# Two-layer encoder in one kernel: the two ends of the seven-product feed-forward cycle in a new order

## Chip, cores and metric

The kernel runs on one core of a Trainium2 chip. The metric is the device time of one launch in microseconds (us). The time before is 1501.56 us, the median of three runs (1500.29, 1501.56 and 1502.72 us).

## The reference, cut to what matters

Two layers over 512 tokens of width 1024. Each layer has three parts, each followed by a layer norm of `ALPHA * x + y`:

```
for l in range(DEPTH):
    y = hybrid_mixer(x, ...)                      # latent attention beside a convolution
    x = layer_norm(ALPHA * x + y, ln1_g[l], ln1_b[l])
    y = memory_cross_attention(x, mem, ...)       # 4 heads of 256, 256 memory tokens
    x = layer_norm(ALPHA * x + y, ln2_g[l], ln2_b[l])
    y = swiglu_ffn(x, ffn_w_in[l], ffn_w_down[l]) # hidden width 2816
    x = layer_norm(ALPHA * x + y, ln3_g[l], ln3_b[l])

def memory_cross_attention(...):
    s = einsum(q, k) * scale;  p = softmax(s);  return einsum(p, v) @ w_o
def swiglu_ffn(x, w_in, w_down):
    g, up = halves of x @ w_in;  return (silu(g) * up) @ w_down
```

## The kernel before, in words

**Numbers.** Every float32 matrix is split into a high and a low part (`split`: ACT writes the high part, DVE subtracts it to get the low part). A product is three matmuls in a row, high by high, low by high, high by low (`mm3`, L250, L251, L252). Tiles named whi, xsh, hs, ph, yx are operands' high parts or pairs, wlo, xsl, pl their low parts.

**Weights.** A raw 512 KB weight tile is fetched by SP (`fetch`) into one of 3 raw buffers. ACT casts it to the high part (L287, L606), ACT writes minus the high part into the low tile (L288, L607), and a DMA issued by POOL adds the raw tensor to it in flight (L289, L608: `wlo<-in_fdn`, `wlo<-in_fin`). There are 7 such pairs of tiles; PSUM has four banks accb, three psb and one convb (every fourth request for a psb bank gets convb).

**Cross attention.** `scores(q, kv)` is 24 matmuls and a softmax on DVE and ACT; `turn(p)` transposes the probabilities on PE (L1242), 8 in all, and splits them (ph, pl); `mix` multiplies them with the values. `first_half(u)`, u = 0 to 3, are the four parts of the first half of the output projection. Before, the order is: scores of head 2, first_half(0), turn of head 2, scores of head 3, first_half(1).

**Feed-forward input.** gate and up are computed in 22 pairs of 128 features (`Pair`), each by seven products instead of eight, on halves of tokens and of width. The token operands are seven: 11 and 21 (`first`) and 22, t1, t2, t4, t3 (`sums`), each made for two chains of token tiles (t = 0 and 1; their halves share one operand tile): t1 = b12 - b11, t2 = b22 - t1, t4 = b21 - t2, t3 = b22 - b12. POOL computes these differences (tsum, L564), PE transposes each in four blocks (`put`, L550), ACT casts (xsh, L225), DVE subtracts (xsl, L226). The weight operands are likewise sums of the pair's gate and up halves (ssum, L619 to L628 on DVE), cast by ACT (L640) with the low part from DVE (L645). A product is 12 matmuls of 256 columns. Its names: p1, p2 (into one accb half), p67, p3, p45; `copy1`, `early_sums`, `late_sums` and `hidden` combine them (DVE), with a tanh on ACT (L688).

`tail_pairs` makes the second half of the attention output, its layer norm (with POOL's ve and rstd, L450, L454) and, in a block of fixed order, the token operands, with p1 and p2 of pairs 0 to 2 between them. `ffn` then runs 22 cycles. In cycle j the sums and casts of pair j+1 are made, and hidden(j-1) is finished.

**Down projection.** For each of 22 feature tiles, `operands(j)` makes the weight tile (`added_weights`) and the hidden tile's split (hs), and `step` issues 24 matmuls of 512 columns (4 token tiles, 2 halves, 3 parts).

**What sets the order.** Inside `with issue_order(...)` the instructions of PE, DVE, ACT, POOL and SP stand in the order in which the code is written; each engine executes its own list in that order, and waits by semaphores. Outside it a scheduler places them by priority. SP's list is a DMA queue of its own, POOL's another.

## Time and profile before

The profiled execution took 1502.71 us. Its span was 1500.9 us, at a mean granted TensorE clock of 0.983.

| engine | busy us | share | instructions |
|---|---|---|---|
| PE (matmul) | 1433.6 | 96% | 9647 |
| DVE | 1023.4 | 68% | 1749 |
| ACT | 804.7 | 54% | 1500 |
| POOL | 500.9 | 33% | 695 |

An engine's busy time is the sum over its instructions. The rest of the span is waiting, and a wait on PE is put down to the instruction whose end released it. PE's busy time also holds matmuls that run at half clock: 0.5 in the column PEclk means 1.2 GHz, 1.0 means 2.4 GHz. The second layer repeats the first about 737.5 us later.

### The profile page before, as it was taken

Reading aid. Unit: us, or ns where it says so; the run is one execution under the profiler, and the core shown is the slowest. Engines: PE = TensorE matmul, PEld = TensorE weight load, DVE = VectorE, ACT = ScalarE, POOL = GpSimd, SP = SyncE. Lnnn points to the kernel's source line nnn. Section 1 sums busy time; section 2 is a strip of 40 time slices with the busy share of each in tenths; the row PEclk is TensorE's granted clock in tenths of the full one; section 3 lists DMA queues with packets and bytes.
Section 4 is the critical chain, followed back from the end, with each engine's and each line's share of the span. In section 5 each row is a group of like instructions: output and inputs, shape, how many; then the busy total and the mean of one; then the engine's idle time right before and its main releaser. Section 6 shows DMA issues by size and latency. Waiting matters only on the chain.

```text
span 1500.9 us, 25060 instructions
## 1 busy us (share of the span) xinstructions
PE 1433.6 (96%) x9647; PEld 1311.2 (87%) x9647; DVE 1023.4 (68%) x1749; ACT 804.7 (54%) x1500; POOL 500.9 (33%) x695
## 2 busy tenths in 40 slices
PE   8899999999799999899999999999997999998997
PEld 8799988988699999888889998888886999997886
DVE  7999677565588888620469986785566888884205
ACT  4667773352356656663146777534415656655630
POOL 2789762001511111211157987410023111111211
PEclk9999999999899999999999999999998999999999
DMA  5434343252477887999433444423525878789971
GB/s 178 152 102 147 108 166 98 94 160 71 112 180 181 183 182 187 256 264 220 120 107 121 141 122 123 150 84 113 155 71 134 194 177 189 181 182 291 252 142 56
DMA packets 68504, 230.67 MB, mean 154 GB/s; under 512 B 7776, under 2 KB 7808, under 8 KB 68384
## 3 DMA queue, kind: packets, MB, share of 16 engines
q1 hardware_dynamic: 45632, 158.09, 32.3%
q0 software_dynamic: 22752, 70.98, 24.9%
q8 instruction: 76, 1.25, 0.3%
q14 instruction: 44, 0.36, 0.1%
HBM read 212.26 MB, written 12.58 MB: 150 GB/s over the span
## 4 chain that ended last, share of the span: by engine, by line
PE 70%; DVE 10%; DMA 7%; ACT 5%; issue 4%; POOL 4%; SPq 0%; POOLq 0%; DVEq 0%; ACTq 0%
PE accb L250 12%; PE accb L251 11%; PE accb L252 11%; PE psb L250 9%; PE psb L251 9%; PE psb L252 9%; DMA raw<-in_xo 3%; PE convb L250 2%; PE convb L252 2%; PE convb L251 2%; DVE convb L844 2%; DMA raw<-in_fdn 1%; DVE wlo L226 1%; POOL tsum L564 1%; DVE p L1074 1%
## 5 line engine op out<-in xcount | busy, mean ns | idle before, releaser
L608 POOL DMA_DIRECT2D wlo<-in_fin x88 | 76.6, 873 | 433.3 <-DVE wlo L645 264.2
L322 POOL TENSOR_TENSOR wlo<-raw,whi 128x1024 fp32r<-128x1024 f32 (+1 forms) x63 | 152.1, 2416 | 59.0 <-ACT whi L314 58.9
L252 PE MATMUL accb<-xsh,wlo 128*128 128x256 f32 x528 | 151.7, 287 | 1.6 <-DMA wlo<-in_fin 1.6
L250 PE MATMUL accb<-xsh,whi 128*128 128x256 f32 x528 | 152.6, 289 | 0.5 <-ACT xsh L225 0.5
L251 PE MATMUL accb<-xsl,whi 128*128 128x256 f32 x528 | 151.7, 287 | 1.2 <-DVE xsl L226 1.2
L251 PE MATMUL psb<-xsl,whi 128*128 128x256 f32 x512 | 145.1, 283 | 2.7 <-DVE xsl L226 2.7
L250 PE MATMUL psb<-xsh,whi 128*128 128x256 f32 x512 | 145.1, 283 | 0.0
L252 PE MATMUL psb<-xsh,wlo 128*128 128x256 f32 x512 | 144.9, 283 | 0.0
L640 ACT CAST whi<-ssum 128x512 fp32r<-128x512 f32 x176 | 99.7, 614 | 72.0 <-DVE ssum L624 60.0
L844 DVE SCALAR_TENSOR_TENSOR convb<-ch,hvec,convb 128x511 f32<-128x511 f32 (+9 forms) x180 | 132.4, 736 | 5.9 <-ACT convb L841 2.0
L250 PE MATMUL accb<-xTh,whi 128*128 128x256 f32 (+1 forms) x352 | 118.4, 340 | 1.4 <-ACT whi L225 1.3
L251 PE MATMUL accb<-xTl,whi 128*128 128x256 f32 (+1 forms) x352 | 118.1, 337 | 0.4 <-DVE xTl L436 0.4
L252 PE MATMUL accb<-xTh,wlo 128*128 128x256 f32 (+1 forms) x352 | 117.7, 335 | 0.4 <-DVE wlo L226 0.4
L226 DVE TENSOR_TENSOR wlo<-raw,whi 128x1024 fp32r<-128x1024 f32 (+1 forms) x43 | 49.3, 1151 | 100.1 <-ACT whi L225 99.3
L645 DVE TENSOR_TENSOR wlo<-ssum,whi 128x512 fp32r<-128x512 f32 x176 | 111.9, 696 | 5.2 <-ACT whi L640 5.1
L252 PEld LDWEIGHTS accb<-xsh,wlo 128*128 128x128 f32 x528 | 103.5, 196 | 2.0 <-DMA wlo<-in_fin 2.0
L251 PEld LDWEIGHTS accb<-xsl,whi 128*128 128x128 f32 x528 | 103.5, 196 | 1.6 <-DVE xsl L226 1.6
L250 PEld LDWEIGHTS accb<-xsh,whi 128*128 128x128 f32 x528 | 103.5, 196 | 1.0 <-ACT xsh L225 1.0
L251 PEld LDWEIGHTS psb<-xsl,whi 128*128 128x128 f32 x512 | 98.3, 192 | 3.1 <-DVE xsl L226 3.1
L289 POOL DMA_DIRECT2D wlo<-in_fdn x44 | 38.1, 866 | 181.1 <-ACT wlo L288 154.5
L250 PEld LDWEIGHTS psb<-xsh,whi 128*128 128x128 f32 x512 | 98.3, 192 | 0.1
L252 PEld LDWEIGHTS psb<-xsh,wlo 128*128 128x128 f32 x512 | 98.3, 192 | 0.0
(348 smaller groups left out, 4672.9 us busy)
## 6 DMA issues: line engine op xcount, KB each, us to landing
raw<-in_fin SPq DMA_DIRECT2D x94, 512.0 KB, 3.8
wlo<-in_fin POOLq DMA_DIRECT2D x44, 512.0 KB, 6.6
raw<-in_fdn SPq DMA_DIRECT2D x44, 512.0 KB, 6.3
wlo<-in_fdn POOLq DMA_DIRECT2D x44, 512.0 KB, 7.8
wlo<-in_fin POOLq DMA_DIRECT2D x44, 256.0 KB, 5.9
raw<-in_xk SPq DMA_DIRECT2D x16, 512.0 KB, 3.6
raw<-in_xv SPq DMA_DIRECT2D x16, 512.0 KB, 3.6
raw<-in_wo SPq DMA_DIRECT2D x16, 512.0 KB, 3.5
```

The source lines that it names most:

```text
L226: nc.vector.tensor_tensor(lo, src, hi.bitcast(F32), op=ALU.subtract)
L250: nc.tensor.matmul(o, l[0], r[0], start=first, stop=False)
L251: nc.tensor.matmul(o, l[0], r[1], start=False, stop=False)
L252: nc.tensor.matmul(o, l[1], r[0], start=False, stop=last)
L289: nc.gpsimd.dma_start(out=lo[:, :1024], in_=src, accum_op=ALU.add)
L322: eng.tensor_tensor(lo, raw, hi.bitcast(F32), op=ALU.subtract)
L564: nc.gpsimd.tensor_tensor(o, a, b, op=ALU.subtract)
L608: nc.gpsimd.dma_start(out=lo, in_=src, accum_op=ALU.add)
L640: nc.scalar.copy(self.w[n][0], self.s[n])
L645: nc.vector.tensor_tensor(lo, self.s[n], hi.bitcast(F32), op=ALU.subtract)
L844: nc.vector.scalar_tensor_tensor(out=o[:, d:], in0=src[:, :SEQ - d], scalar=tap(m, d), in1=o[:, d:], op0=ALU.mult, op1=ALU.add)
L1074: nc.vector.tensor_scalar(p[:, blk(i, nk)], p[:, blk(i, nk)], ri[:, i:i + 1], None, op0=ALU.mult)
```

## The change

The change has four parts, in both layers alike:

- **Cross attention.** The scores of head 3 are issued ahead of the transposes of head 2.
- **Token operands.** The two chains of token sums are made on two engines: chain 0 on POOL (its t1 already while the norm of token tile 3 is being made), chain 1 on DVE. p1 and p2 of pairs 0 and 1 stand in a row ahead of the first token transposes of the block. The weight sums of pair 1 go from DVE to POOL, sum4 of pair 0 goes forward to the first token tile.
- **Pair 2.** The cast and negation of pair 2's gate, and its accumulating DMA, are issued earlier.
- **Last cycle.** Three raw tiles of the down weights are fetched inside cycle 20. Weight tiles and hidden splits 0 to 2 are made inside cycle 21 (`lead`), after tanh of pair 20, and the down projection takes them from there. In SP's list eight down-weight tiles now stand ahead of the loads of x, not six.

```
--- before.py
+++ after.py
@@ -279,9 +279,9 @@
                 split(raw[:, sl], hi[:, sl], lo[:, sl])
         return hi[:, :n], lo[:, :n]
 
-    def added_weights(src):
-
-        raw = fetch(src)
+    def added_weights(src, raw=None):
+
+        raw = fetch(src) if raw is None else raw
         hi = wring.tile([P, 1088], F32R, name="whi")
         lo = wring.tile([P, 1088], F32R, name="wlo")
         nc.scalar.copy(hi[:, :1024], raw[:, :1024])
@@ -558,29 +558,31 @@
         def sums(self, x, t):
 
             b11, b21, b12, b22 = (x[i][:, blk(h, 512)] for i in (t, t + 2) for h in range(2))
-
-            def less(a, b):
-                o = scr(name="tsum")[:, :512]
-                nc.gpsimd.tensor_tensor(o, a, b, op=ALU.subtract)
-                return o
-
-            self.put("22", b22, t)
-            yield
-            t1 = less(b12, b11)
-            self.put("t1", t1, t)
-            yield
-            t2 = less(b22, t1)
-            self.put("t2", t2, t)
-            yield
-            self.put("t4", less(b21, t2), t)
-            yield
-            self.put("t3", less(b22, b12), t)
-            yield
+            made = {"22": b22}
+            room = []
+
+            def less(name, eng, late=True):
+                a, b = {"t1": (b12, b11), "t2": (b22, made.get("t1")), "t4": (b21, made.get("t2")),
+                        "t3": (b22, b12)}[name]
+                if not late:
+                    o = scr(name="tsum")[:, :512]
+                else:
+                    if not room:
+                        pair = bigt([P, 2, 512], F32, name="tsum")
+                        room.extend((pair[:, 0], pair[:, 1]))
+                    o = room.pop(0)
+                eng.tensor_tensor(o, a, b, op=ALU.subtract)
+                made[name] = o
+
+            def put(name):
+                self.put(name, made.pop(name) if name in ("22", "t3", "t4") else made[name], t)
+
+            return less, put
 
     class Pair:
 
 
-        spare = None
+        spare, s = None, None
 
         def __init__(self, gate, up):
             self.gate, self.up, self.ops, self.w = gate, up, {}, {}
@@ -616,12 +618,12 @@
             self.slot("22", "s1")
             self.added(*self.w["22"], self.b[:, 512:1024], self.up[:, 512:1024])
 
-        def sums(self):
+        def sums(self, eng=nc.vector):
             a0, b0, b1 = self.a[:, 0:512], self.b[:, 0:512], self.b[:, 512:1024]
             self.s = {n: scr(name="ssum")[:, :512] for n in ("s1", "s2", "s3")}
-            nc.vector.tensor_tensor(self.s["s1"], b0, b1, op=ALU.add)
-            nc.vector.tensor_tensor(self.s["s2"], self.s["s1"], a0, op=ALU.subtract)
-            nc.vector.tensor_tensor(self.s["s3"], a0, b0, op=ALU.subtract)
+            eng.tensor_tensor(self.s["s1"], b0, b1, op=ALU.add)
+            eng.tensor_tensor(self.s["s2"], self.s["s1"], a0, op=ALU.subtract)
+            eng.tensor_tensor(self.s["s3"], a0, b0, op=ALU.subtract)
 
         def sum4(self):
             self.s["s4"] = scr(name="ssum")[:, :512]
@@ -708,6 +710,10 @@
                 pairs[0].sums()
                 pairs[0].hi("s3", "s2")
                 pairs[0].lo("s3", "s2")
+                pairs[0].sum4()
+            if t == 3:
+                less0, put0 = xs_.sums(x, 0)
+                less0("t1", nc.gpsimd, late=False)
             norm = Norm(x[t], gb)
             o = mm(t)
             for i, y in enumerate(half0(t) + o):
@@ -716,34 +722,40 @@
                 xs_.first(x, t - 2)
             norm.finish(lambda rows, cols: keep(t, rows, cols))
         with issue_order(tc, ORDERED):
-            early, late = xs_.sums(x, 0), xs_.sums(x, 1)
+            less1, put1 = xs_.sums(x, 1)
             pairs[2].fetch_gate()
-            pairs[0].p1(xs_)
-            pairs[0].copy1()
-            pairs[0].sum4()
-            pairs[1].p1(xs_)
-            pairs[1].copy1()
-            next(early)
             pairs[2].split_gate()
             pairs[1].fetch_gate()
-            next(early)
-            pairs[0].p2(xs_)
+            pairs[1].fetch_up()
+            for i in range(2):
+                pairs[i].p1(xs_)
+                pairs[i].copy1()
             pairs[0].split_up()
-            next(early)
-            pairs[1].fetch_up()
-            pairs[2].fetch_gate()
-            next(early)
-            pairs[1].p2(xs_)
-            next(early)
             pairs[0].hi("s1", "s4")
-            pairs[0].lo("s1", "s4")
+            for i in range(2):
+                pairs[i].p2(xs_)
+            for name in ("t2", "t4", "t3"):
+                less0(name, nc.gpsimd)
+            put0("22")
+            less1("t1", nc.vector)
+            less1("t2", nc.vector)
+            put0("t1")
             pairs[2].p1(xs_)
             pairs[2].copy1()
-            for _ in range(2):
-                next(late)
+            less1("t4", nc.vector)
+            put0("t2")
+            put1("t2")
+            less1("t3", nc.vector)
             pairs[2].p2(xs_)
-            for _ in range(3):
-                next(late)
+            put0("t3")
+            put1("t3")
+            put1("22")
+            pairs[1].sums(nc.gpsimd)
+            pairs[0].lo("s4", "s1")
+            for p in (put0, put1):
+                p("t4")
+            put1("t1")
+            pairs[2].fetch_gate()
         return xs_
 
 
@@ -1281,8 +1293,8 @@
         ws.append(moving(xo[l, 0, 0]))
         p2 = scores(q.pop(2), kv[2])
         first_half(0)
+        p3 = scores(q.pop(3), kv[3])
         pp2 = turn(p2)
-        p3 = scores(q.pop(3), kv[3])
         first_half(1)
         mix(kv.pop(2), pp2)
         pp3 = turn(p3)
@@ -1313,6 +1325,17 @@
 
         def dst(j):
             return hid[j // 2][:, j % 2, :]
+
+        raws, ready = [], {}
+
+        def lead(j):
+            ready[j] = operands(j)
+
+        def operands(j):
+            w = added_weights(fdn[l, j], raws.pop(0) if raws else None)
+            hs = pair_tile("hs")
+            split(hid[j // 2][:, j % 2, :], hs[0], hs[1])
+            return w, hs
 
         with issue_order(tc, ORDERED):
             for j in range(NJ):
@@ -1327,8 +1350,11 @@
                     before.late_sums(dst(j - 1))
                 pair.p67(xs_)
                 if after:
-                    after.sums()
+                    if after.s is None:
+                        after.sums()
                     after.hi("s3", "s2")
+                else:
+                    lead(0)
                 if before:
                     before.hidden(dst(j - 1))
                 pair.early_sums()
@@ -1336,7 +1362,11 @@
                     after.sum4()
                     after.hi("s1")
                     after.lo("s3", "s2")
+                else:
+                    lead(1)
                 pair.p3(xs_)
+                if not after:
+                    lead(2)
                 if j + 2 < NJ:
                     pairs[j + 2].fetch_up()
                 if j + 3 < NJ:
@@ -1352,23 +1382,19 @@
                     if j + 1 >= 3:
                         after.copy1()
                 pair.p45(xs_)
+                if j + 2 == NJ:
+                    raws.extend(fetch(fdn[l, i]) for i in range(3))
             pairs[NJ - 1].late_sums(dst(NJ - 1))
             pairs[NJ - 1].hidden(dst(NJ - 1))
         gb = load_gb(l, 2)
         x = load_x(xm)
         o = [[accb() for _ in range(NT)], [psb() for _ in range(NT)]]
 
-        def operands(j):
-            w = added_weights(fdn[l, j])
-            hs = pair_tile("hs")
-            split(hid[j // 2][:, j % 2, :], hs[0], hs[1])
-            return w, hs
-
         def step(j, t, half, w, hs):
             mm3(o[half][t], cut(hs, ALL, blk(t)), cut(w, ALL, blk(half, 512)), j == 0, j == NJ - 1)
 
         for j in range(NJ - RESIDENT):
-            w, hs = operands(j)
+            w, hs = ready.pop(j, None) or operands(j)
             for t in range(NT):
                 for half in range(2):
                     step(j, t, half, w, hs)
```

Where it moves instructions, first POOL at the end of `tail_pairs` in the first layer. x_3343, x_3345, x_3347 and x_3349 are token tiles 0 to 3; the xm row is the store of a normed tile. Before:

```order
L450 TENSOR_SCALAR ve_4660<-mv_4658 128x1
L454 TENSOR_TENSOR rstd_4662<-ve_4660,mhalf_97 128x1
L1302 DMA xm_124<-x_3349 128x1024
L608 DMA wlo_4711<-in_fin 128x1024
L564 TENSOR_TENSOR tsum_4717<-x_3347,x_3343 128x512
L608 DMA wlo_4741<-in_fin 128x512
L564 TENSOR_TENSOR tsum_4745<-x_3347,tsum_4717 128x512
L564 TENSOR_TENSOR tsum_4760<-x_3343,tsum_4745 128x512
L564 TENSOR_TENSOR tsum_4783<-x_3347 128x512
L564 TENSOR_TENSOR tsum_4822<-x_3349,x_3345 128x512
L564 TENSOR_TENSOR tsum_4843<-x_3349,tsum_4822 128x512
L564 TENSOR_TENSOR tsum_4852<-x_3345,tsum_4843 128x512
```

and now:

```order
L574 TENSOR_TENSOR tsum_4616<-x_3347,x_3343 128x512
L450 TENSOR_SCALAR ve_4664<-mv_4662 128x1
L454 TENSOR_TENSOR rstd_4666<-ve_4664,mhalf_97 128x1
L1314 DMA xm_124<-x_3349 128x1024
L610 DMA wlo_4713<-in_fin 128x512
L574 TENSOR_TENSOR tsum_4745<-x_3347,tsum_4616 128x512
L574 TENSOR_TENSOR tsum_4745<-x_3343,tsum_4745 128x512
L574 TENSOR_TENSOR tsum_4748<-x_3347 128x512
L624 TENSOR_TENSOR ssum_4840<-raw_4680 128x512
L625 TENSOR_TENSOR ssum_4841<-ssum_4840,raw_4678 128x512
L626 TENSOR_TENSOR ssum_4842<-raw_4678,raw_4680 128x512
```

Of eight differences four are left on POOL, one of them ahead of the norm's ve of the last tile, and the three sums of pair 1's weights (ssum) stand behind them.

DVE at the same place, before, from the end of the norm (L477) to the low parts:

```order
L628 TENSOR_TENSOR ssum_4684<-raw_4456,ssum_4461 128x512
L477 SCALAR_TENSOR_TENSOR x_3349<-x_3349,rstd_4662,gb_4131 128x1024
L226 TENSOR_TENSOR xsl_4702<-psb_4703,xsh_4701 128x4x128
L226 TENSOR_TENSOR xsl_4720<-psb_4721,xsh_4719 128x4x128
L226 TENSOR_TENSOR xsl_4748<-psb_4749,xsh_4747 128x4x128
L226 TENSOR_TENSOR xsl_4763<-convb_4764,xsh_4762 128x4x128
L226 TENSOR_TENSOR xsl_4786<-psb_4787,xsh_4785 128x4x128
L645 TENSOR_TENSOR wlo_4741<-ssum_4460,whi_4740 128x512
L645 TENSOR_TENSOR wlo_4796<-ssum_4684,whi_4795 128x512
L226 TENSOR_TENSOR xsl_4702<-psb_4815,xsh_4701 128x4x128
```

and now:

```order
L477 SCALAR_TENSOR_TENSOR x_3349<-x_3349,rstd_4666,gb_4131 128x1024
L226 TENSOR_TENSOR xsl_4751<-psb_4752,xsh_4750 128x4x128
L574 TENSOR_TENSOR tsum_4759<-x_3349,x_3345 128x512
L574 TENSOR_TENSOR tsum_4759<-x_3349,tsum_4759 128x512
L226 TENSOR_TENSOR xsl_4763<-psb_4764,xsh_4762 128x4x128
L574 TENSOR_TENSOR tsum_4786<-x_3345,tsum_4759 128x512
L226 TENSOR_TENSOR xsl_4789<-psb_4790,xsh_4788 128x4x128
L226 TENSOR_TENSOR xsl_4789<-convb_4797,xsh_4788 128x4x128
L574 TENSOR_TENSOR tsum_4786<-x_3349 128x512
L226 TENSOR_TENSOR xsl_4818<-psb_4819,xsh_4817 128x4x128
L226 TENSOR_TENSOR xsl_4818<-psb_4826,xsh_4817 128x4x128
```

DVE makes chain 1's four differences (L574) between the low parts (xsl) of the token operands. The operand of p2 of pair 2 is xsl_4789: both its halves stand behind the third difference.

ACT at the end of the cycles, from the copy of p1 of pair 21 (L658; now L660) on, before:

```order
L658 COPY one_7516<-accb_7501 128x256
L287 CAST whi_7688<-raw_7686 128x1024
L288 ACTIVATE wlo_7689<-whi_7688 128x1024
L287 CAST whi_7722<-raw_7720 128x1024
L288 ACTIVATE wlo_7723<-whi_7722 128x1024
L688 ACTIVATE scr_7557<-accb_7378 128x512
L287 CAST whi_7756<-raw_7754 128x1024
L288 ACTIVATE wlo_7757<-whi_7756 128x1024
L287 CAST whi_7790<-raw_7788 128x1024
L287 CAST whi_7824<-raw_7822 128x1024
L288 ACTIVATE wlo_7791<-whi_7790 128x1024
L288 ACTIVATE wlo_7825<-whi_7824 128x1024
```

and now:

```order
L660 COPY one_7513<-accb_7498 128x256
L690 ACTIVATE scr_7560<-accb_7375 128x512
L287 CAST whi_7587<-raw_7539 128x1024
L288 ACTIVATE wlo_7588<-whi_7587 128x1024
L225 CAST hs_7592<-hid_4873 128x512
L287 CAST whi_7600<-raw_7541 128x1024
L288 ACTIVATE wlo_7601<-whi_7600 128x1024
L225 CAST hs_7605<-hid_4873 128x512
L287 CAST whi_7620<-raw_7543 128x1024
L287 CAST whi_7753<-raw_7751 128x1024
L288 ACTIVATE wlo_7621<-whi_7620 128x1024
L225 CAST hs_7625<-hid_4874 128x512
```

The casts of the first three down tiles, which stood ahead of tanh of pair 20 (L688; now L690), stand behind it, and the hidden tile (hs) of each follows its negation.

## Rows read from the trace of the kernel before

**Rows 1.** The page's part 4: shares of the chain that ended last, by engine.

```profile
PE 70%; DVE 10%; DMA 7%; ACT 5%; issue 4%; POOL 4%; SPq 0%; POOLq 0%; DVEq 0%; ACTq 0%
```

**Rows 2.** Waits of PE over the span: us in total, times, longest.

```profile
PE psb L550 <- POOL tsum L564: 14.0, 4, 5.2
...
PE accb L250 <- ACT hs L225: 11.3, 2, 6.6
```

**Rows 3.** Timeline of PE, first layer, cross attention: start, us, instruction [idle before <-releaser].

```profile
328.32 0.39 PE L252 MATMUL accb<-whi,yx 128*128 128x512 f32 x1
...
330.44 0.59 PE L1242 MATMUL psb<-ident,p 128*128 128x128 f32 x2 [1.74 <-DVE p L1233]
...
337.11 0.39 PE L250 MATMUL accb<-whi,yx 128*128 128x512 f32 x1
```

**Rows 4.** Timeline of DVE, same place.

```profile
328.14 1.21 DVE L226 TENSOR_TENSOR kvl<-raw,kvh 128x1024 fp32r<-128x1024 f32 x1
```

**Rows 5.** Windows: span, busy per engine, granted clock, DMA share, GB/s.

```profile
334.00:336.00 2.00, 2.00 (x11) 2.00 (x11) 1.13 (x3) 0.00 (x0) 0.00 (x0) 0.50 0.75 225
...
390.00:400.00 10.00, 4.33 (x20) 3.81 (x20) 0.69 (x1) 3.02 (x5) 5.48 (x5) 0.66 0.90 234
```

**Rows 6.** Timeline of PE, second layer, cross attention.

```profile
1069.43 0.59 PE L1242 MATMUL psb<-ident,p 128*128 128x128 f32 x2
...
1071.30 0.60 PE L1242 MATMUL convb<-ident,p 128*128 128x128 f32 x4
...
1071.66 0.36 PE L250 MATMUL psb<-kvh,xq 128*128 128x256 f32 x1
...
1074.61 0.40 PE L250 MATMUL accb<-whi,yx 128*128 128x512 f32 x1
```

**Rows 7.** Timeline of PE, first layer, token operands after the attention output.

```profile
387.61 0.60 PE L550 MATMUL psb<-ident,x 128*128 128x128 f32 x4
...
393.42 1.12 PE L550 MATMUL psb<-ident,tsum 128*128 128x128 f32 x4 [5.21 <-POOL tsum L564]
...
398.89 0.66 PE L550 MATMUL psb<-ident,tsum 128*128 128x128 f32 x4 [1.79 <-POOL tsum L564]
...
410.88 0.39 PE L251 MATMUL psb<-xsl,whi 128*128 128x256 f32 x1 [1.34 <-DVE xsl L226]
```

**Rows 8.** Timeline of POOL, same place.

```profile
391.76 1.60 POOL L564 TENSOR_TENSOR tsum<-x 128x512 f32<-128x512 f32 x1
```

**Rows 9.** Timeline of POOL and DVE, second layer.

```profile
1142.82 1.28 POOL L564 TENSOR_TENSOR tsum<-x 128x512 f32<-128x512 f32 x1
...
1143.00 2.25 DVE L645 TENSOR_TENSOR wlo<-ssum,whi 128x512 fp32r<-128x512 f32 x2
```

**Rows 10.** Line 645 (DVE): duration ns min/median/max.

```profile
L645 DVE TENSOR_TENSOR wlo<-ssum,whi x176: 677/684/1778, 352.5 to 1353.7; 128x512 fp32r<-128x512 f32 x176
```

**Rows 11.** Timeline of PE, start of the down projection, both layers.

```profile
631.58 0.80 PE L250 MATMUL accb<-whi,hs 128*128 128x512 f32 x1 [4.67 <-ACT hs L225]
...
639.51 0.39 PE L250 MATMUL accb<-whi,hs 128*128 128x512 f32 x1
...
1370.94 0.80 PE L250 MATMUL accb<-whi,hs 128*128 128x512 f32 x1 [6.58 <-ACT hs L225]
```

**Rows 12.** Timeline of ACT before it, first layer.

```profile
620.33 0.58 ACT L688 ACTIVATE scr<-accb 128x512 f32<-128x512 f32 x1
...
628.07 1.04 ACT L287 CAST whi<-raw 128x1024 fp32r<-128x1024 f32 x1 [2.47 <-DMA raw<-in_fdn]
...
630.93 2.16 ACT L225 CAST hs<-hid 128x512 fp32r<-128x512 f32 x4
...
633.00 0.58 ACT L688 ACTIVATE scr<-accb 128x512 f32<-128x512 f32 x1
```

**Rows 13.** DMA issues of 600 to 650: KB each, median us to landing.

```profile
wlo<-in_fdn POOLq DMA_DIRECT2D x7, 512.0 KB, 14.9
```

**Rows 14.** Window at the down projection.

```profile
636.00:646.00 10.00, 10.00 (x44) 8.24 (x43) 2.51 (x5) 0.49 (x1) 0.00 (x0) 0.97 1.05 274
```

## The prediction

> **What bounds the kernel now.** I read the chain of waits first, then PE's waits, then the timelines and windows where these fall. TensorE ends 70% of the chain, VectorE 10%, DMA 7%, ScalarE 5%, POOL 4% [rows 1], so a shorter wait of PE shortens the run and other work mostly does not. The reader is to see that two of PE's waits stand out and that each falls at an end of the feed-forward cycle: 14.0 us in four waits for POOL's token sums, and 11.3 us in two waits for the split of hidden tiles on ScalarE [rows 2]. Waits also cost afterwards: in 390 to 400 us PE was busy 4.33 of 10 us and the granted clock was 0.66, in 334 to 336 it was 0.50, the 1.2 GHz level [rows 5]. Both layers do the same, so each term counts twice, with its own rows where they differ.
>
> **Cross attention (scores ahead of the turn).** In the first layer first_half(0) ends in a matmul that starts at 328.32 and the next part starts at 337.11 [rows 3]. That matmul holds PE for about 0.23 (an estimate: 512 columns where 24 matmuls of 256 take 2.95, below), so 8.56 us lie between 328.55 and the next part. Between stand a wait of 1.74 for the probabilities [rows 3], a second one, and scores that ran at half clock [rows 5]. At full clock the 24 score matmuls take 1074.61 - 1071.66 = 2.95, and a set of four transposes 1071.66 - 1071.30 = 0.36, two sets with change-over 0.8 [rows 6]. Now the scores go first. They need the low part of the keys, ready at 328.14 + 1.21 = 329.35 [rows 4], so 0.8 of wait stays; the softmax of head 2 then runs under the scores and its transposes find p ready. 0.8 + 2.95 + 0.8 = 4.55, a gain of 4.0. In the second layer there was no half clock and the keys are early: 1074.61 - 1069.43 = 5.18 [rows 6] against 3.75, a gain of 1.4. What is late next is the mix of head 2: DVE and ACT make its operands behind head 3's softmax, which might cost back 0 to 1 a layer. Term: 5.4, bounds 3 and 6.5.
>
> **Token operands.** Before, PE needs from 387.61 to 410.76 (the row at 410.88 less the one matmul ahead of its wait), 23.15 us [rows 7], for four products of 12 matmuls (p2 of pairs 0 and 1, p1 and p2 of pair 2) and ten sets of transposes. Work alone is 4 x 1.47 (half of 2.95) + 10 x 0.4 = 9.9. The rest is the waits of 5.21 and 1.79 [rows 7], a smaller one, low parts at the end, and half clock.
>
> Now p2 of pairs 0 and 1 come at once after 387.61: 390.55. The sets 22(0) and t1(0) need no new sum (t1 was made under the norm of the last tile): 391.35. p1 of pair 2, whose weights were issued far ahead, ends at 392.8, t2(0) at 393.2. POOL's t2 can begin about 390.6, against 391.76 for its first sum before [rows 8], because what it waits for on ScalarE is half as wide; its six operations then follow at 1.28 each [rows 9]. VectorE's four differences would take 0.68 each if they ran freely [rows 10]: t1(1) from 392.2, t2(1) done at 393.6. In that case p2 of pair 2 runs from 394.2, and the last sets, still waiting some 1.2 in all for t3(1) and t1(1), end so that p67 of pair 0 starts at 399.55. That would be a gain of 11.2.
>
> But the trace has a row against it. At 1142.82 POOL starts a difference of 1.28, ending 1144.10; at 1143.00 VectorE starts two subtractions of two SBUF operands, and they take 2.25 where two take 1.36 [rows 9, 10]: 0.89 late, or nearly to the end of POOL's operation and then at its own speed. The longest of 176 such subtractions is 1.78, one operation of 0.68 and one POOL operation of the free length less a little [rows 10]. So I take them as excluding each other and taking turns. The Trainium skill (SBUF — State Buffer, section "SBUF: two separate sides") says that GpSimd and a VectorE operation with two SBUF inputs share one port pair as an exclusive lock, held for the whole instruction. Here the trace agrees (0.89 of lateness beside 1.28). By durations alone this term would be 22.4, by the rule 16 before the clock.
>
> In turns: POOL's second operation ends 393.15, t1(1) 393.8, POOL 395.1, t2(1) 395.8, POOL 397.1, t4(1) 397.8. The low parts of p2's token operand stand behind t4(1) on VectorE (the order shows it) and take 2 x 0.68 more: 398.9 or so (their input from PSUM leaves them free of POOL). p2 of pair 2 ends 400.4, six sets of transposes 402.8. Gain 410.76 - 402.8 = 8.0. PE is then nearly idle from 393.2 to 398.9, as it was from 388 to 393.4 before, where the clock fell [rows 5, 7]; p2 at half clock costs 1.47 more and the sets behind it up to as much. I take 1.5 off: 6.5 a layer, 13 in both. Bounds 4 and 11.2 a layer. The sums of pair 1, now POOL's last, end near 401, ahead of their use after p67 of pair 0; POOL's t1 stands where POOL waited for the norm of the last tile, ahead of ve. Both cost nothing there; if t1 held up ve it would cost at most its 1.28.
>
> **Last cycle.** Before, the down projection starts at 631.58 after a wait of 4.67, and its second tile at 639.51 [rows 11]. 24 matmuls of 0.228 (the estimate above) are 5.47, so the 12.6 us from the end of p45 (631.58 - 4.67 = 626.9) to 639.51 hold 7.1 of loss. The hidden splits are queued on ScalarE behind casts that wait for a raw tile (2.47 at 628.07): they start at 630.93 [rows 12]. Now the splits of tiles 0 to 2 come ahead of that wait, but their casts stand behind tanh of pair 20, which ends at 620.9 [rows 12]. Then ScalarE needs for a tile a cast of 1.04, a negation of about the same and a split of 2.16 / 4 = 0.54 [rows 12], some 2.7 with change-over: hs0 is ready at 623.6, and hs2, behind one more cast of tile 3, at about 630. p45 starts 1 late, because the sums on VectorE stand behind the first split. The DMA that completes low weight tile 0 is issued about 623, behind that tanh and no longer ahead of it. The wait for raw tiles 4 and 5 remains ahead of tanh of pair 21, which the fourth accb bank needs; it ran at 633.00 [rows 12], and with the casts of three more tiles between the two tanhs I put it at 636. I place the point that answers to 639.51 at 636.8: gain 2.7, and 3.6 in the second layer, whose wait was 6.58 [rows 11]. Term: 6.3. Bounds: -2 (late tiles eat it all) and 15 (no loss left in either layer).
>
> The Trainium skill (DMA: Bandwidth & Descriptors, section "Issuing engines are not separate DMA queues") says that transfers of all issuing engines run on the same 16 DMA engines and interleave, so that issuing elsewhere saves only the issue. The DMA share here is 1.05 [rows 14], which agrees; by that rule the term is near 0.
>
> **Sum.** 5.4 + 13 + 6.3 = 24.7. The profiled execution took 1502.71, 1.15 above the median of the runs shown; 1502.7 - 24.7 = 1478.0 in its terms, 1477 in the median's. The likeliest case alone reaches from 1469 to 1486.
>
> **Rivals.**
> 1. *POOL and VectorE do not exclude each other*, or POOL's gaps let VectorE in: the token term is 22.4, time 1467.5. For it: POOL's chained differences leave gaps. Against: the 2.25 [rows 9].
> 2. *The down projection gives nothing back*: its start is bound by the accumulating DMAs, 14.9 from issue to landing there [rows 13], or by tanh of pair 21. Tile 0's low part issued at 623 lands at 637.9, and the first tile cannot end before. Term 0: 1483. Against: the median of 14.9 holds the x loads' worst moments.
> 3. *Slower*: the down projection starves. The casts start behind the tanh and two loads more go ahead of x; PE's lead over the accumulating DMAs was what kept it at 10.00 of 10 us from 636 on [rows 14]. If only two of these transfers of 14.9 [rows 13] overlap until x has landed, a tile takes 7.45 instead of 5.47, six tiles cost 12 a layer, 24 in both: 1501.6 - 18.4 + 24 = 1507. It decides from 9.2 a layer on. Against: the wide DMA rate, 274 GB/s [rows 14], moves a tile's 1 MB in 3.9.
> 4. *The clock stays low and the turns lengthen*: token term at its bound of 4 a layer, 8; time 1482.
>
> **Chances.** Forecast 0.48, rival 1 0.20, rival 2 0.16, rival 4 0.10, rival 3 0.06. A measurement tells apart about 0.2%, 3 us. Of the first, second and fourth all are faster; with something of rivals 2 and 4 together at 1488 still faster. Faster 0.92, same 0.02, slower 0.06. Range: 1461 to 1490, which leaves out the best of all bounds (6.5, 22.4, 15: 1458) and rival 3.
>
> **What would show it.** Cross attention: the waits of L1242 gone, no half clock at 334. Token operands: VectorE's differences lasting up to 1.9 beside POOL's, PE's wait at the fourth or fifth set of transposes, p67 of pair 0 about 8 earlier after the first p2 than before. Without lengthened differences rival 1 is right. Last cycle: no wait of 4.67, instead waits of L251 for wlo or of the fourth accb bank. The forecast is wrong if PE waits for wlo tile after tile behind the start, or if the token stretch takes over 20 us.

## The result, and the profile after

The changed kernel takes 1479.05 us (median of four runs, 1478.26 to 1481.22), against 1500.92 before in the same count of runs; the ratio is 0.9858, 95% interval 0.9839 to 0.9878. Forecast were 1477 and the range 1461 to 1490. The profiled execution's span fell from 1500.9 to 1477.9, by 23.0 us, the granted clock rose from 0.983 to 0.992.

The waits of TensorE that answer to [rows 2] (us in total, times, longest):

```profile
PE convb L550 <- DVE tsum L574: 4.6, 2, 2.3
...
PE accb L250 <- DVE scr L695: 4.3, 2, 2.5
...
PE accb L251 <- DMA wlo<-in_fdn: 3.5, 2, 2.1
PE psb L550 <- DVE tsum L574: 3.2, 2, 2.1
```

The wait for POOL's sums and the wait for the hidden splits are gone. In their place stand waits for VectorE's sums, for a low weight tile's DMA, and for tanh of pair 21 (L695 is the VectorE instruction behind it that frees the last accb bank).

Where the time went, read as differences of the same landmarks in both timelines:

| stretch | forecast | measured, layers 1 and 2 | sum |
|---|---|---|---|
| cross attention to the end of the second half | 5.4 | 4.75, 1.44 | 6.2 |
| from there to p67 of pair 0 | 13 | 6.65, 7.86 | 14.5 |
| the 22 cycles | 0 | 0.7, 0.5 | 1.2 |
| start of the down projection | 6.3 | 1.7, 1.1 | 2.9 |
| mixer of the second layer | 0 | -2.0 | -2.0 |

The remaining 0.3 lies ahead of the first landmark. A landmark is the start of a named matmul: for the down projection its hundredth, where both kernels run without a wait, and for p67 of pair 0 before, which holds a wait behind its first matmul, the point that the prediction took, 410.76.

**Cross attention.** TensorE, to be read beside [rows 3]:

```profile
328.02 0.39 PE L252 MATMUL accb<-whi,yx 128*128 128x512 f32 x1
328.24 0.28 PE L250 MATMUL psb<-kvh,xq 128*128 128x256 f32 x1
...
331.12 1.04 PE L1254 MATMUL psb<-ident,p 128*128 128x128 f32 x8
331.91 0.48 PE L250 MATMUL accb<-whi,yx 128*128 128x512 f32 x1
```

The last matmul of first_half(0), then the 24 scores without a wait, eight transposes, the next part: 3.89 us instead of 8.79. The 0.8 of wait that the forecast left did not come, because in this execution VectorE had the low part of the keys ready at 327.58, 1.8 earlier than in [rows 4]. In other executions part of it does come: in the kernel called tanh_first below, with the same order here, TensorE waits 0.6 for that low part in the second layer, and the stretch takes 4.72.

**Token operands.** VectorE's four differences (with two low parts, xsl, between the third and the fourth) and POOL's six operations; t2(1) is the sum t2 of chain 1:

```profile
387.32 1.52 DVE L574 TENSOR_TENSOR tsum<-x 128x512 f32<-128x512 f32 x1
388.88 1.64 DVE L574 TENSOR_TENSOR tsum<-x,tsum 128x512 f32<-128x512 f32 x1
...
391.04 1.17 DVE L574 TENSOR_TENSOR tsum<-x,tsum 128x512 f32<-128x512 f32 x1
392.13 0.68 DVE L226 TENSOR_TENSOR xsl<-psb,xsh 128x512 fp32r<-128x512 f32 x1
392.73 0.67 DVE L226 TENSOR_TENSOR xsl<-convb,xsh 128x512 fp32r<-128x512 f32 x1
393.32 1.80 DVE L574 TENSOR_TENSOR tsum<-x 128x512 f32<-128x512 f32 x1
```

```profile
385.30 3.00 POOL L574 TENSOR_TENSOR tsum<-x,tsum 128x512 f32<-128x512 f32 x2
388.26 1.71 POOL L574 TENSOR_TENSOR tsum<-x 128x512 f32<-128x512 f32 x1
389.93 1.73 POOL L624 TENSOR_TENSOR ssum<-raw 128x512 f32<-128x512 f32 x1
391.73 1.61 POOL L625 TENSOR_TENSOR ssum<-ssum,raw 128x512 f32<-128x512 f32 x1
393.31 1.26 POOL L626 TENSOR_TENSOR ssum<-raw 128x512 f32<-128x512 f32 x1
```

Most of these operations are longer than their free length of 0.68 or 1.28 [rows 9, 10], and the two lists interlock: t1(1) starts at 387.32, while POOL's pair of 385.30 to 388.30 still runs, and ends at 388.84, 0.54 after that pair; POOL's next starts at 388.26, while t1(1) still runs, takes 1.71 and ends 1.13 after it. An operation that starts while one runs on the other engine is longer by about the rest of that one, and the one that started first mostly keeps its length: POOL's last takes 1.26 beside the difference of 1.80. POOL's first pair is another matter. It takes 3.00 instead of 2.56, but 3.01 in two kernels below as well, where no VectorE operation with two SBUF operands runs beside it.

TensorE in the same stretch (first transposes after the second half, then as in [rows 7]):

```profile
377.46 0.60 PE L550 MATMUL psb<-ident,x 128*128 128x128 f32 x4
...
387.76 0.60 PE L550 MATMUL psb<-ident,tsum 128*128 128x128 f32 x4
390.66 0.63 PE L550 MATMUL convb<-ident,tsum 128*128 128x128 f32 x4 [2.30 <-DVE tsum L574]
391.04 0.36 PE L250 MATMUL accb<-xsh,whi 128*128 128x256 f32 x1
...
393.07 1.05 PE L550 MATMUL psb<-ident,tsum 128*128 128x128 f32 x4
395.27 1.08 PE L550 MATMUL psb<-ident,tsum 128*128 128x128 f32 x4 [1.14 <-DVE tsum L574]
...
399.07 0.36 PE L250 MATMUL psb<-xsh,whi 128*128 128x256 f32 x1
```

The two waits are for the sums t2(1) and t3(1). The product at 391.04 is p2 of pair 2. It runs right behind the transposes of t2(1) and ahead of the low parts of 392.13 and 392.73, so these are not its operand. The sentence ahead of the prediction that calls xsl_4789 the operand of p2 of pair 2 is wrong: that tile is t2, which p67 reads, while p2 reads operand 21 (in the code `PARTNER` gives "21" for "12" and "t2" for "s2"), made by `first` before this block.

From 377.46 to 399.07 it is 21.61, where before it was 410.76 - 382.50 = 28.26. The windows of the two layers (columns as in [rows 5]), 729.0 us apart like the ends of the second half:

```profile
392.00:398.00 6.00, 4.86 (x23) 4.49 (x23) 4.55 (x7) 1.75 (x3) 2.57 (x2) 0.50 0.30 90
1121.00:1127.00 6.00, 3.81 (x31) 3.19 (x31) 5.17 (x8) 2.67 (x6) 2.55 (x2) 1.00 0.31 90
```

In the first layer the clock fell to 0.50 behind the wait of 2.30, in the second it stayed at 1.00 in the corresponding stretch, with the same instructions behind the same wait of 2.30; there the wait for t3(1) was 2.10 instead of 1.14. That leaves 1.2 of difference between the layers (6.65 and 7.86).

**Down projection.** TensorE and ScalarE at its start, the answer to [rows 11, 12]:

```profile
611.46 0.40 PE L250 MATMUL accb<-whi,hs 128*128 128x512 f32 x1
...
618.85 0.50 PE L251 MATMUL accb<-wlo,hs 128*128 128x512 f32 x1 [2.14 <-DMA wlo<-in_fdn]
...
625.45 0.50 PE L250 MATMUL accb<-whi,hs 128*128 128x512 f32 x1 [1.82 <-DVE scr L695]
```

```profile
623.13 1.05 ACT L287 CAST whi<-raw 128x1024 fp32r<-128x1024 f32 x1 [2.96 <-DMA raw<-in_fdn]
624.08 0.59 ACT L690 ACTIVATE scr<-accb 128x512 f32<-128x512 f32 x1
```

TensorE begins tile 0 at 611.46, between p3 and p45 of the last pair, on the six high products that have banks and operands. It then waits 2.14 for the low weight tile, issued about 610.5, and 1.82 for the bank that tanh of pair 21 sets free. That tanh ran at 624.08, directly behind a cast that waited 2.96 for a raw tile. In the second layer the two waits are 1.33 and 2.48. Behind the 2.48 the clock is lower, behind the 1.82 of the first layer it is not:

```profile
1353.26 0.50 PE L250 MATMUL accb<-whi,hs 128*128 128x512 f32 x1 [2.48 <-DVE scr L695]
```

```profile
625.00:629.00 4.00, 3.56 (x16) 2.95 (x17) 1.08 (x2) 2.50 (x3) 1.71 (x2) 1.00 1.03 335
1353.00:1357.00 4.00, 3.74 (x11) 2.99 (x12) 0.90 (x2) 2.42 (x3) 1.71 (x2) 0.68 1.03 342
```

**Mixer of the second layer.** The 2.0 lost here lie in two places. About 0.7 comes with a wait of 0.51 for a tile of the memory at 791.24, which the trace before has not. The other 1.3 is the clock: the same 14 matmuls, behind the same wait of 1.0 for the mixer's probabilities (L1074 before, L1086 now), take 1.76 before and 3.06 now:

```profile
931.35:933.11 1.76, 1.76 (x14) 1.68 (x13) 1.73 (x5) 1.40 (x2) 0.22 (x1) 1.00 0.80 221
```

```profile
918.20:921.26 3.06, 3.06 (x14) 2.98 (x14) 2.96 (x6) 1.89 (x6) 1.73 (x3) 0.55 0.78 255
```

### The profile page after: what moved, and what is told of

Read it like the earlier page. It is cut to its first block, busy times and chain, and to the rows that moved or that the text cites. A ratio compares the mean times of both kernels' runs of the same rounds, so it can differ in the third digit from the quotient of the medians.

```text
span 1477.9 us, 25063 instructions
## 1 busy us (share of the span) xinstructions
PE 1426.3 (97%) x9647; PEld 1303.6 (88%) x9647; DVE 1028.0 (70%) x1751; ACT 804.5 (54%) x1500; POOL 497.4 (34%) x693
## 4 chain that ended last, share of the span: by engine, by line
PE 74%; DVE 6%; issue 6%; POOL 6%; DMA 4%; ACT 4%; SPq 0%; POOLq 0%; DVEq 0%; ACTq 0%
PE accb L250 12%; PE accb L251 12%; PE accb L252 12%; PE psb L252 9%; PE psb L250 9%; PE psb L251 9%; PE convb L250 2%; PE convb L251 2%; PE convb L252 2%; POOL wlo L322 2%; DMA raw<-in_fdn 1%; DVE convb L856 1%; DVE p L1086 1%; PE psb L1091 1%; DMA wlo<-in_fin 1%
```

## The experiments

Each result is the median, the ratio to before with its 95% interval, and what the trace shows.

**Each part alone.** Three kernels, each with the hunks of one part of the diff on the kernel before.

Cross attention alone: 

> Only the scores of head 3 ahead of the turn of head 2; all else as before. Theory (the parts act one beside the other): the cross-attention stretch is shorter by 4.9 us in the first layer and 1.5 in the second, as between the two profiles, so about 6.4 off the time before: 1494.5. Rival (part of the 4.9 came from the transfers of that run and not from the order): by the predicted 4.0 and 1.4, 1495.5, with a wait of about 0.8 for the low part of the keys at the first score. Second rival (the 2.0 us lost in the second layer's mixer come with this part): 1496.5.

1498.06 us, 0.9978 (0.9964 to 0.9993), so 3.3 us, between 1.1 and 5.4. The profile has the full gain of the stretch (3.89 in both layers); the median has about half of it. In the profile 1.1 of that gain is lost again by the hundredth matmuls of the two down projections, whose waits for the hidden splits grew from 11.3 to 12.9.

Token operands alone: 

> Only the token sums in two chains, the four products in a row, pair 2's weights earlier, pair 1's sums on POOL. Theory: 6.6 and 7.9 us in the token stretch and 1.3 in the cycles behind it, 15.8 off the time before: 1485. VectorE's four differences last 1.2 to 1.8 beside POOL's. Rival (the 2.0 us lost in the second layer's mixer come with this part): 1487.

1486.02 us, 0.9892 (0.9873 to 0.9912), 16.2 us. p67 of pair 0 comes 20.4 after the end of the second half in the first layer and 21.5 in the second: here the shorter one is the first. The mixer lost 0.4 in this trace, not 2.0.

Last cycle alone: 

> Only the last cycle: weights and hidden tiles 0 to 2 made in it. Theory: 1.7 and 1.1 us at the start of the down projection, so 2.9 off the time before: 1498, with PE waiting about 2 us for the low weight tile 0 and about 2 for tanh of pair 21. Rival (the start of the down projection is bound by transfers that this part only makes later): 1500 to 1502. If the 2.0 us lost in the second layer's mixer come with this part, it shows in the same stretch here and the time is 1500.

1498.22 us, 0.9976 (0.9963 to 0.9988), 3.6 us. The waits were the forecast ones, 3.1 for low weight tiles and 3.8 for tanh of pair 21. The three parts alone give 3.3 + 16.2 + 3.6 = 23.1, the change as a whole 0.0142 of 1501, 21.3: they add up within their intervals. The stretch in the mixer from the hundredth matmul to the second layer's output projection is 407.4 in the trace before and 407.4, 407.9 and 408.7 in these three, and, in the changed kernel and the eight that follow here, 407.4 to 408.1 in four and 409.0 to 409.5 in the rest, with the same instructions of the mixer in all. It goes with no part of the change but with the clock of those 14 matmuls: 1.00 in the seven traces of 407.4 to 408.1, 0.50 to 0.56 in the six of 408.7 to 409.5, behind the same wait of 1.0 in all thirteen. Why the clock falls in some executions stays open.

**Do POOL and VectorE exclude each other?**

The first of four lines; `less` then subtracts half of pair 0's accb bank and reads one operand from SBUF:

```
-            less1("t1", nc.vector)
+            less1("t1", nc.vector, v=pairs[0].v)
...
```

> The changed kernel, but each of VectorE's four differences takes its subtrahend from PSUM (the first half of pair 0's accb, broadcast) and not from SBUF, so it has one SBUF input; POOL's work is the same. The values of chain 1 are therefore other ones. Theory (VectorE and POOL exclude each other when both read two SBUF operands): the four differences go back to about 0.7 each, p67 of pair 0 starts 3 to 5 us earlier in each layer, 1470 to 1473. Rival (their 1.2 to 1.8 is VectorE's own: waiting for its own results, or the operation's cost there): they stay long, and the time stays at 1479.

1473.04 us, 0.9804 (0.9781 to 0.9827), for a kernel that leaves out chain 1's true sums. VectorE's four differences beside the same POOL operations:

```profile
388.20 0.68 DVE L578 TENSOR_TENSOR tsum<-x,accb 128x512 f32<-128x512 f32 x1
388.92 0.69 DVE L578 TENSOR_TENSOR tsum<-tsum,accb 128x512 f32<-128x512 f32 x1
...
390.12 0.68 DVE L578 TENSOR_TENSOR tsum<-tsum,accb 128x512 f32<-128x512 f32 x1
...
391.92 0.67 DVE L578 TENSOR_TENSOR tsum<-x,accb 128x512 f32<-128x512 f32 x1
```

All are back at 0.67 to 0.69, and POOL's are at 1.26 to 1.29 behind the first pair of 3.01. From the end of the second half to p67 of pair 0 it takes 17.0 us in both layers, 11.2 less than before: the very number that the prediction worked out for a VectorE that runs freely (and took for the rival). So the length of the differences comes from a second SBUF operand beside a POOL operation, not from the operation. The other half of the proof stands below, in the kernel with the differences made early: two of them with both operands in SBUF, but with no POOL arithmetic beside them, take 0.69 each. This is what the Trainium skill (SBUF — State Buffer, section "SBUF: two separate sides") states of the shared port pair; the runs agree, with 1.17 to 1.80 where both operands are in SBUF and 0.67 to 0.69 where one is in PSUM.

**Chain 1 back on POOL.**

```
-            less1("t1", nc.vector)
+            less1("t1", nc.gpsimd)     # t2, t4, t3 likewise
...
```

> The changed kernel with chain 1's four differences on POOL, at the same places in the code; VectorE makes none. Theory (VectorE and POOL take turns, so chain 1 on VectorE saves little over a single queue): POOL has t2, t4, t3 of chain 0, then four more and three sums, 1.28 each; t2(1) is ready some 1.3 us later than now, t3(1) about as now; p67 of pair 0 within 2 us of the changed kernel in each layer, 1476 to 1482. Rival (the second engine is what the token part gains by): four differences more in POOL's queue delay the chain by 4 to 5 us a layer, 1487 to 1489.

1479.71 us, 0.9865 (0.9845 to 0.9885): the changed kernel's time. POOL runs at free length but for the first pair, which takes 3.01 with VectorE idle or on low parts from PSUM:

```profile
385.63 3.01 POOL L574 TENSOR_TENSOR tsum<-x,tsum 128x512 f32<-128x512 f32 x2
388.59 2.48 POOL L574 TENSOR_TENSOR tsum<-x 128x512 f32<-128x512 f32 x2
391.15 2.62 POOL L574 TENSOR_TENSOR tsum<-x,tsum 128x512 f32<-128x512 f32 x2
```

PE waits longer for t2(1) (3.8 instead of 2.3) and not at all for t3(1). The second engine for the sums gains nothing as it stands. What the token part gains must then come from the rest of it: the products in a row, t1 under the norm, pair 2's weights early, pair 1's sums on POOL. These were not run apart, so how they share it is not shown.

**Differences where POOL is silent.**

```
+            for name in ("t1", "t2", "t4", "t3"):
+                less1(name, nc.vector)        # ahead of POOL's t2, t4, t3 and of put0("22")
...
```

> The changed kernel with VectorE's four differences written ahead of the low part of operand 22, so that they fall into the 2.95 us in which VectorE waits for ScalarE and POOL issues DMAs. Theory (turns): t1(1) and t2(1) take 0.7 each there, t4(1) and t3(1) meet POOL's t2 at most; from the end of the second half to p67 of pair 0 it takes 16 to 17.5 us (21.6 and 20.4 in the changed kernel, 17.0 with the PSUM operand), 1470 to 1472. Rival (the stretch is bound by POOL's chain 0 or by the low parts): 20 us or more and 1478 to 1480.

1469.65 us, 0.9798 (0.978 to 0.9815), 9 us below the changed kernel. VectorE, and the window:

```profile
383.95 0.69 DVE L574 TENSOR_TENSOR tsum<-x 128x512 f32<-128x512 f32 x1
384.68 2.97 DVE L574 TENSOR_TENSOR tsum<-x,tsum 128x512 f32<-128x512 f32 x2
387.57 1.76 DVE L574 TENSOR_TENSOR tsum<-x 128x512 f32<-128x512 f32 x1
```

```profile
386.00:392.00 6.00, 5.83 (x51) 5.62 (x50) 5.87 (x7) 3.32 (x8) 5.84 (x5) 1.00 0.60 178
```

t1(1) and t2(1) are free (0.69 each, the second inside the pair of 2.97); t4(1), the other 2.24 of the pair, and t3(1) still meet POOL's. But their late ends no longer stand in front of anything: TensorE is busy 5.83 of 6, the clock stays at 1.00, and the stretch is 16.2 in both layers.

**The start of the down projection.** Two kernels, each against one wait.

```
# early_w: casts, negations, DMAs of tiles 0 and 1 ahead of tanh of pair 20
...
+                if not after:
+                    for i in range(2):
+                        early[i] = added_weights(fdn[l, i], raws.pop(0))
                 if before:
                     before.late_sums(dst(j - 1))
# tanh_first: tile 3 ahead of, tiles 4 and 5 behind tanh of pair 21, in fixed order
...
+            early[3] = added_weights(fdn[l, 3])
             pairs[NJ - 1].late_sums(dst(NJ - 1))
             pairs[NJ - 1].hidden(dst(NJ - 1))
+            for i in (3, 4, 5):
+                lead(i)
```

> The changed kernel with the casts, negations and accumulating DMAs of down tiles 0 and 1 ahead of tanh of pair 20, in ScalarE's wait of 4.2 us; the hidden splits stay where they are. Theory (the first product waits for low weight tile 0, whose DMA is issued too late): the waits for wlo of 2.1 and 1.3 go, 3 us in both layers less what tanh of pair 21 then holds up, 1476 to 1477.5. Rival (the start is set by tanh of pair 21 and by the fourth accb bank): the wait moves to that bank, 1479.

1478.28 us, 0.9853 (0.9837 to 0.9869): no gain. The wait for wlo went, and the other grew from 4.3 to:

```profile
PE accb L250 <- DVE scr L695: 7.9, 2, 4.0
```

> The changed kernel with tiles 3 to 5 of the down projection inside the block of fixed order, so that tanh of pair 21 stands ahead of the casts of tiles 4 and 5, which wait for their raw tiles; tile 3's weights stay ahead of it. Theory (the fourth accb bank waits for that tanh behind raw tiles): tanh of pair 21 runs about 4.5 us earlier, the waits of 1.8 and 2.5 for it go, 4 us in both layers: 1475. Rival (the accumulating DMAs set the start, all else hides behind them): the waits turn into waits for wlo of tiles 1 to 4, 1478 to 1480.

1473.38 us, 0.9815 (0.9794 to 0.9836). tanh of pair 21 and the cast that had held it up:

```profile
618.06 0.60 ACT L690 ACTIVATE scr<-accb 128x512 f32<-128x512 f32 x1 [0.66 <-DVE accb L688]
...
626.47 1.05 ACT L287 CAST whi<-raw 128x1024 fp32r<-128x1024 f32 x1 [2.75 <-DMA raw<-in_fdn]
```

The wait for the bank is gone; 2.3 for low weight tiles are left, where it was 3.5. So of the two waits in a row the removal of the earlier one (early_w) gained nothing, and that of the later one gained 5.7 us of medians.

**Together.** First the early differences and the early tanh of pair 21 in one kernel:

> The changed kernel with early1 and tanh_first together. Theory (the two ends are separate, each with its own wait): early1's 9.4 and tanh_first's 5.7 add up, 15 off the changed kernel's 1479: 1464 (1462 to 1466). Rival (what the second gives was luck of its runs or is given back by late weight tiles): 1468 to 1470.

1462.23 us, 0.9745 (0.9728 to 0.9761): they add up.

Then the early weights of tiles 0 and 1 in addition:

> All three: early1, tanh_first and early_w. Theory (early_w alone only moved PE's wait from low weight tile 0 to the fourth accb bank, from 2.1 to 4.0; with tanh of pair 21 ahead of the waiting casts that bank is free in time): the waits for wlo that tanh_first left (2.3 in all) go too, 1.5 to 2.5 below early1_tanh, 1461 to 1463. Rival (the DMA engines are full there, so earlier issues only put off later tiles): no difference to early1_tanh.

1457.37 us, 0.9722 (0.9706 to 0.9737). With that tanh out of the way early_w seems to count, by 3.5 us of ratios and 4.9 of medians (the intervals still overlap a little); its trace has none of the 2.4 of waits for low weight tiles that the kernel without it has. TensorE at the start of the down projection:

```profile
608.00:612.00 4.00, 4.00 (x25) 3.51 (x24) 1.83 (x4) 1.29 (x3) 1.43 (x2) 1.00 1.03 269
620.00:624.00 4.00, 4.00 (x19) 3.31 (x18) 0.69 (x1) 2.16 (x3) 2.22 (x3) 1.00 1.04 319
```

It is busy throughout, at full clock, with no wait there in either layer. This version beats both kernels: 2.8% below before, 21.7 us below the changed kernel.

**How much is the cross-attention part?**

```
-        p3 = scores(q.pop(3), kv[3])
         pp2 = turn(p2)
+        p3 = scores(q.pop(3), kv[3])
```

> The changed kernel with the scores of head 3 behind the turn of head 2, as before; all else as in the changed kernel. Theory (part of the 4.9 of the first layer was the half clock of the profiled execution of before, which the token part's own profile did not show: there the same stretch took 5.65 us without the reordering, against 8.79 before and 3.89 in the changed kernel): the reordering is worth 1.8 and 1.5, 3.3 in all, 1482 to 1483. Rival (the half clock comes in most executions, so the full 6.4 count): 1485.

1482.93 us, 0.9863 (0.9838 to 0.9888), runs from 1479.73 to 1486.63. By medians the reordering is worth 3.9 on top of the rest, by ratios 0.7 with an interval of some 5. The half clock was there in this profile (stretch 8.59), which I had not expected, and absent in that of the token part alone (5.65), with the same order. Of the four profiles with the old order, three have it in the first layer: before (8.79), the last cycle alone (8.50) and this one. First this profile, then that of the token part alone:

```profile
333.00:335.00 2.00, 2.00 (x11) 2.00 (x11) 1.90 (x3) 1.17 (x2) 0.00 (x0) 0.50 0.00 0
```

```profile
333.00:335.00 2.00, 2.00 (x17) 1.91 (x17) 1.11 (x2) 0.79 (x3) 0.00 (x0) 1.00 0.76 250
```

So one order gives two times for this stretch. Four profiles are too few to tell in which share of executions the clock falls; the profiles (6.2) are the upper end for this part, the timed run alone says 1 to 5.

## Why the prediction was right, and where a term was off

- **What bounds the kernel.** Right: with PE's two large waits and those in the cross attention taken away the span fell by 23 us, while VectorE's busy time rose from 1023.4 to 1028.0.
- **Cross attention, 5.4.** Mechanism right: no wait, no half clock, and little late in the mix behind it (0.16). The profile gave 6.2, the timed run alone 3.3 (1.1 to 5.4): the term rested on the half clock of one execution, which comes in three of four profiles with the old order, and on a full gain of which the run alone lost part at the down projection. One figure's working is off, without consequence: 2.95 for 24 matmuls of 256 columns gives 0.246 for one of 512, not 0.23 or 0.228; the timelines do show about 0.23 from one such matmul to the next.
- **Token operands, 13.** The mechanism, taking turns, is right, and the choice between the two ends, 11.2 and 8.0, was decided by the one row of 2.25 [rows 9]; the PSUM operand shows that it was the right row. In the prediction's own stretch, which starts 5.1 behind the end of the second half, the 23.15 became 16.5 and 15.3. But one step of the replay was false: it had p2 of pair 2 wait for the low parts behind t4(1), until 398.9. They are t2's, which p2 does not read. p2 ran right behind the transposes of t2(1), at 391.04 here, which is 396.1 in the prediction's times. In place of those low parts TensorE waited for t3(1), the last difference, for which the replay by turns had no wait. By the prediction's own turns t3(1) would have ended near 401 and p67 started near 403 (an estimate: POOL's sixth operation to 400.4, the difference 0.68, five sets of 0.4), beside its 402.8. So the false step cost nothing, and that the layer with a full clock gave 7.86 beside 8.0 is in part luck. The clock was charged 1.5 in each layer and cost 1.2 in one and nothing in the other. By the Trainium skill (SBUF — State Buffer, section "SBUF: two separate sides") the prediction put 16 for both layers ahead of the clock; 15.7 is twice the layer whose clock held. What the prediction did not see is that, placed as here, the turns make the second engine worth nothing (chain 1 on POOL costs the same).
- **Last cycle, 6.3.** The mis-sized term: 2.9 in the profiles, 3.6 (1.8 to 5.6) alone. The waits are the named ones, and tanh of pair 21 came where it was put (636 forecast, 624.08 + 12.4 of earlier gain = 636.5). The step that was off is the place given to the second tile, 636.8, and its copy for the second layer: both waits were paid one after the other, 2.14 and 1.82, and in the second layer, behind its 2.48, the clock fell (0.68 in the 4 us behind it), so there it was 1.1, not 3.6. The prediction took from the Trainium skill (DMA: Bandwidth & Descriptors, section "Issuing engines are not separate DMA queues") that all transfers share the same 16 DMA engines, and from that a term near 0. The section speaks of issuing from several engines, and here the same engine issues earlier, so it does not give the time of this term. The DMA share is 1.03 and 1.04 in the windows of the last kernel, so those engines were full there; what was gained was waits at the start, not transfer time.
- **The total.** 24.7 forecast and 23.0 measured in the span are nearer than the terms. Cross attention, token operands and cycles gave 3.5 more than forecast, the last cycle 3.4 less, and the mixer, put at nothing, took 2.0. So the forecast total is in part luck. The 1.2 of the 22 cycles was not forecast either, and no run ties it to a part: with the cross attention alone, where the cycles are those of before, the second layer's are 0.6 shorter too.
- **Rivals.** Free VectorE (1467.5): refuted for this kernel, confirmed as a price for the stretch by the PSUM operand (17.0, the worked-out 11.2 less). Clock low and longer turns (1482): the clock did fall in the first layer, but the term there was 6.65, not 4. Nothing from the last cycle (1483): half right, by its own mechanism of tanh and low tile. Starving down projection (1507): PE was busy 10.00 of 10 us from the hundredth matmul on, so no.

## What to carry to other kernels

Before work goes to a second engine, look in the trace for a place where the two already overlap with the same operand kinds: one row of 2.25 where 1.36 was due told the size of this term. Put such work where the other engine is silent, or give it a PSUM operand, rather than beside it. When replaying an order by hand, look up in the code which operand each product reads: a tile name in the order does not tell. And where two waits stand in a row on the bounding engine, removing the earlier one can lengthen the later one by as much, as here (3.5 gone, 3.6 more); see which instruction is queued behind a wait for a transfer (here a tanh behind casts) and move both.

## What the runs showed of the hardware

- A VectorE difference of 128 x 512 with two SBUF operands took 0.69 us with no POOL arithmetic beside it and 1.17 to 2.24 beside POOL; with one operand in PSUM 0.67 to 0.69, beside the same POOL work. POOL's 1.28 grew to 1.74 in turn.
- The same instructions after similar waits left the granted clock at 1.00 in one layer and at 0.50 in the other, and the same stretch of the cross attention ran at 0.50 in one profile and at 1.00 in another. In the mixer of the second layer 14 matmuls behind a wait of 1.0 us ran at 1.00 in seven traces and at 0.50 to 0.56 in six.
